# First layer's attention of a two-layer decoder: rows of two blocks, scores ahead of their maxima, group 2's factor in its probabilities

## The chip, the cores and the metric

The kernel runs on one core of one Trainium2 chip as one launch. The metric is the device time of the launch in microseconds, the median of the runs shown. The engines are called by the names of the profile: PE (TensorE: matmuls; PEld: its weight loads), DVE (VectorE), ACT (ScalarE), POOL (GpSimd) and SP (SyncE, which issues most transfers). Each takes its own instructions in the order of the program and waits on the others by semaphores. Matmul results land in PSUM, of which there are eight banks of 512 floats per partition here; everything else lives in SBUF.

## The reference, cut to what matters

The trunk has two layers on a residual stream of 512 rows and 1024 columns. The change touches the attention of the first layer alone: twelve heads of 64 in three groups of four. Group 0 sees the 128 rows before, group 1 takes every fourth row, group 2 every sixteenth. Each group has its own softmax, and the groups are weighed against each other by their softmax denominators.

```python
def banded_attention(q, k, v, n_back):
    ...
    s = jnp.where(mask[None, :, None], s, NEG)
    m = jnp.max(s, axis=-1, keepdims=True)
    p = jnp.exp(s - m)
    l = jnp.sum(p, axis=-1, keepdims=True)
    o = jnp.einsum('nbhqk,nbkhd->nbqhd', (p / l).astype(v.dtype), vc)
    lse = (m + jnp.log(l))[..., 0]

def dilated_mixer(xn, w_qkv, w_o, cos, sin):
    ...
    alpha = jax.nn.softmax(jnp.stack(lses, axis=0), axis=0)
    o = jnp.concatenate([outs[g] * alpha[g][..., None].astype(outs[g].dtype)
                         for g in range(len(A_GROUPS))], axis=2)
    return o.reshape(B, T, A_WIDTH) @ w_o
```

## The kernel before

Large products run as three matmuls each on a number split into a high and a low part (lines 290 to 292, `mm3`); the high part is a copy on ACT, the low part a subtraction on DVE. Weights are loaded by SP, split ahead of use (`W`, lines 60 and 78, or 64 and 82 where a gain is multiplied in), and taken in order.

The attention is worked through in four projections one after the other. `v_proj0` makes group 0's values. `wide_proj(1, ...)` and `wide_proj(2, ...)` make queries and keys of groups 1 and 2, and a last `wide_proj` the values of both. A `wide_proj` holds four PSUM banks from its start to its end, one for each block of 128 rows, and runs four rounds of 24 matmuls. Behind each round a row of a table names what is put between the rounds: this table is the order of the work. Four banks are left for everything in the rows:

- `qk_transpose(g, b)`: four transposes of the queries and keys of block b into a bank (qkT_ps), copied to SBUF by DVE.
- `scores(g, b)`: for each half `hh` of the heads a bank (s_ps) with two heads' scores (lines 1141 and 1143; K is 64, so the two halves lie on different rows of PE's array), then for each head `softmax`: one DVE instruction scales, masks and takes the maximum (line 1126), one ACT instruction takes the exponential and its sum (line 1127). The probabilities are in `p`, the statistics in `st`.
- `p_transpose(g, b)`: the probabilities of a block transposed into a bank (pT_ps, line 1163) and copied to SBUF by ACT.
- `next(sums)`, `next(down0)`: a step of another job, four DVE subtractions (dsums, lines 593 to 596) that prepare the down projection's weights, with their loads and stores on SP.

`factors` (line 1187 on) works out each group's weight from the statistics and spreads each group's factor to 64 columns (`fac`, line 1198: DVE for group 0, POOL for groups 1 and 2). Behind the last projection comes what is called the tail here: `pv` multiplies probabilities and values (o_ps, lines 1212 and 1215; 64 output rows a head, two halves of the array side by side), and ACT copies the result to SBUF (`ow`); `weigh` transposes the factor (f_ps, line 1228) and DVE multiplies (line 1230); `combine` splits the product into high and low part (OT, lines 1236 and 1237). Groups 1 and 2 are kept in the regrouped order of rows until `pv` copies them back. The tail ends where the output projection begins (acc, `Proj`), which takes eight banks and group 0's OT first, groups 1 and 2 some 11 us later; in its middle it calls `late`.

Of the kernel before, what the change touches and what calls it, by code (L numbers as in the profile page):

```python
# [9 lines left out]
F32 = mybir.dt.float32  # L10
F32R = mybir.dt.float32r
BF16 = mybir.dt.bfloat16
AF = mybir.ActivationFunctionType
# [104 lines left out]
def trunk_kernel(ctx, tc, x, norm_gains, w_qkv_a, w_o_a, w_q_b, w_o_b, kv_norm, w_kvf, b_f,  # L118
# [1007 lines left out]
        dve.tensor_tensor_reduce(p, s, mask, -0.125, BIG, ALU.add, ALU.min, keep[:, hd:hd + 1])  # L1126
        act.activation(p, p, AF.Exp, bias=keep[:, hd:hd + 1], scale=-1.0, accum_out=keep[:, 4 + hd:5 + hd])

    def scores(g, b):
        q = qkT[g]  # L1130

        k0 = 0 if (g == 0 and b) else 1
        n = 256 if g == 0 else 128
        p = None
        for hh in range(2):
            hs_ = slice(64 * hh, 64 * hh + 64)
            o = bank([128, 2, n], name="s_ps")
            for pr in range(2):
                if g == 0:
                    ov = o[:, pr, k0 * 128:].rearrange("p (k c) -> p k c", c=128)  # L1140
                    pe.matmul(ov, q[hs_, b, pr, :], q[hs_, b - 1 + k0:b + 1, 2 + pr, :], start=True, stop=True)
                else:
                    pe.matmul(o[:, pr, :], q[hs_, b, pr, :], q[hs_, b, 2 + pr, :], start=True, stop=True)
            if g == 0 or hh == 0:
                p = t2([128, 512 // n, n], name="p")
                P[g, b, hh] = p
            for pr in range(2):
                if g == 0:
                    softmax(g, b, 2 * pr + hh, o[:, pr, k0 * 128:], mask0[:, k0 * 128:], p[:, pr, k0 * 128:])
                else:  # L1150
                    softmax(g, b, 2 * pr + hh, o[:, pr, :], mask0[:, 128:256] if g == 1 else mask2,
                            p[:, 2 * hh + pr, :])

    def p_transpose(g, b):
        if b == 0:
# [25 lines left out]
    def factors():  # L1181
# [11 lines left out]
        dve.tensor_tensor(mn, mn, w[:, 2], ALU.add)  # L1193
        dve.reciprocal(mn, mn)
        dve.tensor_tensor(f, f, mn[:, None].to_broadcast([128, 3, 4, 4]), ALU.mult)
        for g in range(3):
            fac[g] = t4([128, 4, 4, HD], name="fac")
            (pool.tensor_copy if g else dve.tensor_copy)(fac[g], f[:, g, :, :, None].to_broadcast([128, 4, 4, HD]))

# [2 lines left out]
    def pv(g, pr):  # L1202
        o = bank([128, T], name="o_ps")
        for b in range(4):
            for hh in range(2):
                hd = 2 * pr + hh
                ov = o[64 * hh:64 * hh + 64, b * 128:(b + 1) * 128]
                vs = slice(hd * 64, hd * 64 + 64)
                if g == 0:
                    ks = [0, 1] if b else [1]  # L1210
                    for k in ks:
                        pe.matmul(ov, V[g][:, b - 1 + k, vs], PT[g][hh][:, b, 2 * pr + k, :],
                                  start=k == ks[0], stop=k == 1)
                else:
                    pe.matmul(ov, V[g][:, b, vs], PT[g][0][:, b, 2 * hh + pr, :], start=True, stop=True)
        ow[g, pr] = t = t2([128, T], name="ow")
        if g == 0:
            act.copy(t, o)
# [13 lines left out]
    def combine(g, pr):  # L1232
        t = ow.pop((g, pr))
        if pr == 0:
            OT[g] = t8([128, 2, 2, T], F32R, name=f"OT{g}")
        act.copy(OT[g][:, 0, pr, :], t)
        dve.tensor_tensor(OT[g][:, 1, pr, :], t, OT[g][:, 0, pr, :].bitcast(F32), ALU.subtract)

    def v_proj0(between):
        banks = []  # L1240
# [160 lines left out]
    v_proj0([[L(qk_transpose, 0, 0), L(qk_transpose, 0, 1), L(next, down0)],  # L1401
             [L(qk_transpose, 0, 2), L(qk_transpose, 0, 3), L(scores, 0, 0), L(scores, 0, 1), L(next, sums), L(next, down0)]])
# [16 lines left out]
    for g in range(2):  # L1419
        for pr in range(2):  # L1420
            pv(g, pr)
    weigh(0, 0)
    weigh(0, 1)
    combine(0, 0)
    pv(2, 0)
    pv(2, 1)
    weigh(1, 0)
    combine(0, 1)
    weigh(1, 1)
    combine(1, 0)  # L1430
    weigh(2, 0)
    combine(1, 1)
    weigh(2, 1)

    rows = load_conv(0)
    grow = t2([16, 128], name="g_rows")
# [3 lines left out]
    cp = []  # L1440

    def late():
        combine(2, 0)
        combine(2, 1)
# [406 lines left out]
```

## Time and profile before

| | us |
|---|---|
| median of three runs | 1103.31 (1102.62 to 1103.96) |
| the profiled execution | 1103.35 |
| its span, first to last instruction | 1101.6 |
| queries and keys of groups 1 and 2, values, with their rows | 47 to 131 |
| the tail, to the first matmul of the output projection | 131 to 141.8 |

All instructions after the output projection are the same in both kernels. The page gives each engine's busy time and the chain that ended last; a timeline lists rows of equal instructions with their start, the time from the first start to the last end, engine, line, operation, what is written and read, and in brackets how long the engine was idle before and what released it. PE's instructions overlap, so that there the distance from one start to the next counts, and not the duration. PE's clock was granted at 0.998 of full speed throughout.

### The profile page before, as it was taken

How to read it: one execution, taken by the hardware profiler on the slowest of the kernel's cores; microseconds unless marked ns; L12 is line 12 of the kernel's file. 1: busy time of each engine (PE TensorE's matmuls, PEld its weight loads, DVE VectorE, ACT ScalarE, POOL GpSimd, SP SyncE). 2: the span in 40 equal slices, each digit the busy share in tenths (PEclk: the TensorE clock that was granted, in tenths of full speed). 3: DMA queues.
4: the chain of work that ended last, by engine and by line, in shares of the span. 5: the costliest groups of instructions: out<-in, count | busy, mean ns of one | idle time of the engine just before them, and what ended most of it. 6: DMA issues, size and time to landing. Idle time of an engine off the chain costs nothing.

```text
span 1101.6 us, 18104 instructions
## 1 busy us (share of the span) xinstructions
PE 1093.7 (99%) x6608; PEld 951.8 (86%) x6608; DVE 877.1 (80%) x1498; ACT 670.4 (61%) x1114; POOL 174.2 (16%) x247
## 2 busy tenths in 40 slices
PE   9999999999999999999999999999999999999997
PEld 6988889899999988888878888889899999988886
DVE  5897788888788679997587667868888788779894
ACT  6754565756666647576552488755656666647572
POOL 3632001311111211000000212101311111211000
PEclk9999999999999999999999999999999999999999
DMA  9799854477987979894446867784468888989872
GB/s 316 205 359 408 312 168 136 90 184 187 212 193 182 247 255 321 306 321 119 134 154 219 268 187 198 233 263 135 87 180 193 206 190 183 238 269 321 308 249 77
DMA packets 192130, 242.67 MB, mean 220 GB/s; under 512 B 12848, under 2 KB 138792, under 8 KB 192040
## 3 DMA queue, kind: packets, MB, share of 16 engines
q1 hardware_dynamic: 176408, 189.33, 53.0%
q0 software_dynamic: 14944, 52.18, 20.7%
q8 instruction: 52, 0.85, 0.3%
q14 instruction: 38, 0.31, 0.1%
q10 hardware_dynamic: 688, 0.01, 0.0%
HBM read 172.37 MB, written 39.73 MB: 193 GB/s over the span
## 4 chain that ended last, share of the span: by engine, by line
PE 97%; DMA 1%; DVE 1%; issue 0%; ACT 0%; DVEq 0%
PE up L292 12%; PE up L291 12%; PE up L290 12%; PE acc L290 9%; PE acc L292 9%; PE acc L291 9%; PE v_ps L292 2%; PE v_ps L290 2%; PE v_ps L291 2%; PE qk_ps L1305 2%; PE pT_ps L1692 2%; PE o_ps L1707 2%; PE s_ps L1658 2%; PE first L292 1%; PE first L290 1%; PE first L291 1%
## 5 line engine op out<-in xcount | busy, mean ns | idle before, releaser
L290 PE MATMUL acc<-w 128*128 128x512 f32 (+1 forms) x311 | 120.6, 388 | 0.3 <-DVE mix L339 0.3
L292 PE MATMUL acc<-w 128*128 128x512 f32 (+1 forms) x311 | 120.4, 387 | 0.0
L291 PE MATMUL acc<-w 128*128 128x512 f32 (+1 forms) x267 | 103.2, 387 | 0.0
L78 DVE TENSOR_TENSOR w<-wraw,w 128x1024 fp32r<-128x1024 f32 x62 | 82.3, 1346 | 22.2 <-ACT w L60 21.8
L292 PE MATMUL up<-xsh,w 128*128 128x256 f32 x352 | 99.7, 283 | 0.1
L290 PE MATMUL up<-xsh,w 128*128 128x256 f32 x352 | 99.6, 283 | 0.0
L291 PE MATMUL up<-xsl,w 128*128 128x256 f32 x352 | 99.6, 283 | 0.0
L627 ACT ACTIVATE bb<-up,conv 128x512 f32<-128x512 f32 x80 | 59.6, 775 | 59.4 <-DVE up L1014 48.6
L60 ACT CAST w<-wraw 128x1024 fp32r<-128x1024 f32 x81 | 83.3, 1049 | 17.3 <-PE v_ps L291 6.9
L291 PE MATMUL up<-xbl,w 128*128 128x512 f32 (+1 forms) x276 | 93.5, 339 | 0.0
L291 PE MATMUL up<-xcl,w 128*128 128x512 f32 (+1 forms) x276 | 93.5, 339 | 0.0
L292 PE MATMUL up<-xbh,w 128*128 128x512 f32 (+1 forms) x276 | 93.5, 339 | 0.0
L290 PE MATMUL up<-xch,w 128*128 128x512 f32 (+1 forms) x276 | 93.5, 339 | 0.0
L290 PE MATMUL up<-xbh,w 128*128 128x512 f32 (+1 forms) x276 | 93.5, 339 | 0.0
L292 PE MATMUL up<-xch,w 128*128 128x512 f32 (+1 forms) x276 | 93.4, 338 | 0.0
L290 PEld LDWEIGHTS acc<-w 128*128 128x128 f32 x311 | 58.4, 188 | 12.4 <-DVE mix L339 0.7
L292 PEld LDWEIGHTS acc<-w 128*128 128x128 f32 x311 | 58.4, 188 | 12.0
L292 PEld LDWEIGHTS up<-xsh,w 128*128 128x128 f32 x352 | 67.6, 192 | 0.3 <-DMA w<-wsum 0.3
L291 PEld LDWEIGHTS up<-xsl,w 128*128 128x128 f32 x352 | 67.6, 192 | 0.0
L290 PEld LDWEIGHTS up<-xsh,w 128*128 128x128 f32 x352 | 67.6, 192 | 0.0
L628 DVE SCALAR_TENSOR_TENSOR bb<-up,conv,bb 128x511 f32<-128x511 f32 x80 | 59.5, 744 | 5.9 <-ACT bb L627 5.8
L630 DVE SCALAR_TENSOR_TENSOR bb<-up,conv,bb 128x510 f32<-128x510 f32 x80 | 59.9, 748 | 2.8
(313 smaller groups left out, 3109.1 us busy)
## 6 DMA issues: line engine op xcount, KB each, us to landing
wraw<-in_w_up_dram SPq DMA_DIRECT2D x88, 512.0 KB
w<-wraw POOLq DMA_DIRECT2D x32, 512.0 KB, 6.4
dT<-dsums SPq DMA_DIRECT2D x28, 512.0 KB
w<-wsum POOLq DMA_DIRECT2D x24, 512.0 KB, 5.7
dsums<-in_w_down_dram SPq DMA_DIRECT2D x22, 512.0 KB
dsums<-in_w_down_dram SPq DMA_DIRECT2D x44, 256.0 KB
hD<-hc POOLq DMA_DIRECT2D x44, 256.0 KB, 6.7
dact<-hD SPq DMA_DIRECT2D x44, 256.0 KB
```

Of the source, the lines that this page charges most:

```text
L60: (copy or self.nc.scalar.copy)(pair[:, 0], raw)
L78: self.nc.vector.tensor_tensor(pair[:, 1], raw, pair[:, 0].bitcast(F32), ALU.subtract)
L290: pe.matmul(o, ah, bh, start=first, stop=False, skip_group_check=shared)
L291: pe.matmul(o, ah, bl, start=False, stop=False, skip_group_check=shared)
L292: pe.matmul(o, al, bh, start=False, stop=last, skip_group_check=shared)
L627: act.activation(bb[:, s, :], ps, AF.Identity, bias=cp[:, 3, ch:ch + 1], scale=cp[:, 2, ch:ch + 1])
L628: dve.scalar_tensor_tensor(bb[:, s, 1:], ps[:, :T - 1], cp[:, 1, ch:ch + 1], bb[:, s, 1:], ALU.mult, ALU.add)
L630: dve.scalar_tensor_tensor(bb[:, s, 2:], ps[:, :T - 2], cp[:, 0, ch:ch + 1], bb[:, s, 2:], ALU.mult, ALU.add)
L1305: pe.matmul(qk_banks[b], a[n == 2], w[n == 1][:, kc % 2, :], start=kc + n == 0, stop=kc + n == KD + 1)
L1658: pe.matmul(sc[j, i][hh][:, :nn], qT[j][own, qp, i * 128:(i + 1) * 128], k[own, kp, :nn], start=qp + kp == 0, stop=qp == 1)
L1692: pe.transpose(o[:, k0 + k, :], p[:, hh, k * 128:(k + 1) * 128], ident)
L1707: pe.matmul(o[64 * hh:64 * hh + 64, i * 128:(i + 1) * 128], Vt[hd // 8][:, k, (hd % 8) * 64:(hd % 8) * 64 + 64], pT[j, i, hh][:, k, :], st ...
```

## The change

- `scores` takes several blocks. All their matmuls are issued first, into banks that for groups 1 and 2 hold both blocks of a half (two banks for two blocks, and not four), and all maxima and exponentials follow.
- The tables put two blocks' scores or two blocks' transposes in a row. The last row of each `wide_proj` is left empty or has no PE work.
- `factors` multiplies group 2's factor into its probabilities `p` (four DVE multiplications of 128x512), and spreads a factor for groups 0 and 1 alone. It stands one row earlier.
- Group 2 is transposed in the tail, its product is not copied to `ow` and not weighed; `combine` splits it straight from PSUM, in regrouped order.
- Group 2's values are scaled and copied by ACT, as group 1's are, and not by DVE.
- The tail's order is new, and `combine(2, ...)` moves from `late` into it.

```diff
-    def scores(g, b):
-        q = qkT[g]
-
-        k0 = 0 if (g == 0 and b) else 1
+    def scores(g, *blocks):
+        q, todo = qkT[g], []
         n = 256 if g == 0 else 128
...
+        if g:
+            both = [bank([128, 2, 2, n], name="s_ps") for _ in range(2)]
+        for b in blocks:
+            k0 = 0 if (g == 0 and b) else 1
+            p = None
+            for hh in range(2):
+                hs_ = slice(64 * hh, 64 * hh + 64)
+                o = both[hh][:, b % 2] if g else bank([128, 2, n], name="s_ps")
...
+                    else:
+                        todo.append((g, b, 2 * pr + hh, o[:, pr, :], mask0[:, 128:256] if g == 1 else mask2,
+                                     p[:, 2 * hh + pr, :]))
+        for a in todo:
+            softmax(*a)
...
-        for g in range(3):
+        for b in range(4):
+            p = P[2, b, 0].rearrange("p (h r) c -> p h r c", h=2)
+            fb = f[:, 2, b].rearrange("p (r h) -> p h r", h=2)[:, :, :, None].to_broadcast([128, 2, 2, 128])
+            dve.tensor_tensor(p, p, fb, ALU.mult)
+        for g in range(2):
             fac[g] = t4([128, 4, 4, HD], name="fac")
             (pool.tensor_copy if g else dve.tensor_copy)(fac[g], f[:, g, :, :, None].to_broadcast([128, 4, 4, HD]))
...
+        if g == 2:
+            ow[g, pr] = o
+            return
         ow[g, pr] = t = t2([128, T], name="ow")
...
-        act.copy(OT[g][:, 0, pr, :], t)
-        dve.tensor_tensor(OT[g][:, 1, pr, :], t, OT[g][:, 0, pr, :].bitcast(F32), ALU.subtract)
+        hi, lo = (OT[g][:, part, pr, :] for part in range(2))
+        if g == 2:
+            t = t.rearrange("p (r l) -> p r l", r=4)
+            hi, lo = (a.rearrange("p (l r) -> p r l", r=4) for a in (hi, lo))
+        act.copy(hi, t)
+        dve.tensor_tensor(lo, t, hi.bitcast(F32), ALU.subtract)
...
-        dve.tensor_scalar(V[2][:, b, :], o[:, 256:512], factor(2, b), None, ALU.mult)
+        act.activation(V[2][:, b, :], o[:, 256:512], AF.Identity, scale=factor(2, b))
...
     wide_proj(1, "qk_ps", qk_post, [
-        [L(p_transpose, 0, 0)],
-        [L(scores, 0, 2), L(scores, 0, 3), L(p_transpose, 0, 1), L(next, sums)],
-        [L(p_transpose, 0, 2), L(next, sums)],
-        [stat_out, L(p_transpose, 0, 3), L(next, sums)]])
+        [L(p_transpose, 0, 0), L(p_transpose, 0, 1)],
+        [L(scores, 0, 2, 3), L(next, sums)],
+        [L(p_transpose, 0, 2), L(p_transpose, 0, 3), L(next, sums)],
+        [stat_out, L(next, sums)]])
...
-        [L(qk_transpose, 1, 2), L(scores, 1, 0), L(scores, 1, 1)],
-        [L(qk_transpose, 1, 3), L(p_transpose, 1, 0)],
-        [L(scores, 1, 2), L(scores, 1, 3), L(p_transpose, 1, 1), stat_in]])
+        [L(qk_transpose, 1, 2), L(qk_transpose, 1, 3), L(scores, 1, 0, 1)],
+        [L(p_transpose, 1, 0), L(p_transpose, 1, 1), L(scores, 1, 2, 3)],
+        [stat_in]])
...
-        [L(qk_transpose, 2, 0), L(qk_transpose, 2, 1), L(p_transpose, 1, 2)],
-        [L(qk_transpose, 2, 2), L(qk_transpose, 2, 3), L(scores, 2, 0), L(scores, 2, 1), L(p_transpose, 1, 3)],
-        [L(scores, 2, 2), L(scores, 2, 3), L(p_transpose, 2, 0)],
-        [factors, L(p_transpose, 2, 1), L(p_transpose, 2, 2), L(p_transpose, 2, 3)]])
-    for g in range(2):
-        for pr in range(2):
-            pv(g, pr)
+        [L(p_transpose, 1, 2), L(p_transpose, 1, 3), L(qk_transpose, 2, 0), L(qk_transpose, 2, 1)],
+        [L(qk_transpose, 2, 2), L(qk_transpose, 2, 3), L(scores, 2, 0, 1)],
+        [L(scores, 2, 2, 3), factors],
+        []])
+    pv(0, 0)
+    pv(0, 1)
     weigh(0, 0)
     weigh(0, 1)
+    for b in range(4):
+        p_transpose(2, b)
     combine(0, 0)
+    pv(1, 0)
+    pv(1, 1)
...
+    combine(1, 0)
     pv(2, 0)
     pv(2, 1)
...
     combine(1, 1)
-    weigh(2, 1)
+    combine(2, 0)
+    combine(2, 1)
```

The first place is PE behind the second round of the value projection (v_ps), where group 2's first scores stand; the numbers behind names are those of the buffers. Before:

```order
L292 MATMUL v_ps<-w,xpl_147 128x512
L1116 MATMUL qkT_ps<-ident,qk_1126 128x128 x8
L1143 MATMUL s_ps<-qkT_1249 128x128 x8
L1163 MATMUL pT_ps<-ident,p 128x128 x4
L290 MATMUL v_ps<-w,xph_146 128x512
```

Now:

```order
L292 MATMUL v_ps<-w,xpl_147 128x512
L1116 MATMUL qkT_ps<-ident,qk_1158 128x128 x8
L1145 MATMUL s_ps<-qkT_1257 128x128 x8
L290 MATMUL v_ps<-w,xph_146 128x512
L291 MATMUL v_ps<-w,xph_146 128x512
```

The transposes of group 1's last probabilities have moved a row ahead; the scores are as many, in two banks.

The second place is DVE between group 2's last maxima and the tail: the factors (f_mn, f_f, f_w), the weight's low part (w), the sums (dsums) and the weighing (ow). Before:

```order
L596 TENSOR_TENSOR dsums<-dsums 128x512
L78 TENSOR_TENSOR w<-wraw,w 128x1024
L1398 TENSOR_SCALAR V_1446<-v_ps,rt 128x256 x4
L1187 TENSOR_TENSOR f_mn<-st 128x16
L1188 TENSOR_TENSOR f_mn<-f_mn,st 128x16
L1189 TENSOR_TENSOR f_f<-f_mn,st 128x48
L1191 TENSOR_TENSOR f_w<-st,f_f 128x48
L1192 TENSOR_TENSOR f_mn<-f_w 128x16
L1193 TENSOR_TENSOR f_mn<-f_mn,f_w 128x16
L1194 RECIPROCAL f_mn<-f_mn 128x16
L1195 TENSOR_TENSOR f_f<-f_f,f_mn 128x48
L1198 COPY fac<-f_f 128x1024
```

Now, from the last step of the factors on:

```order
L1199 TENSOR_TENSOR f_f<-f_f,f_mn 128x48
L1203 TENSOR_TENSOR p<-p,f_f 128x512 x4
L1206 COPY fac<-f_f 128x1024
L593 TENSOR_TENSOR dsums<-dsums 128x512
L594 TENSOR_TENSOR dsums<-dsums 128x512
L595 TENSOR_TENSOR dsums<-dsums 128x512
L596 TENSOR_TENSOR dsums<-dsums 128x512
L78 TENSOR_TENSOR w<-wraw,w 128x1024
L1241 TENSOR_TENSOR ow<-ow,f_ps 128x4x128 x2
L1252 TENSOR_TENSOR OT_1551<-ow,OT_1551 128x512 x2
```

The factors come ahead of the sums and the low part, with four multiplications of p ahead of the copy, and the values of group 2 are gone from DVE.

The third place is PE in the tail, from the end of group 0's products. Before (twelve transposes of group 2's probabilities stand ahead of group 0's products):

```order
L1212 MATMUL o_ps<-PT_1_676,V_507 64x128 x2
L1215 MATMUL o_ps<-PT_0_1096,V_1445 64x128 x16
L1228 MATMUL f_ps<-ident,fac 128x128 x8
L1215 MATMUL o_ps<-PT_0_1421,V_1446 64x128 x16
L1228 MATMUL f_ps<-ident,fac 128x128 x16
L290 MATMUL acc<-w,OT_1579 128x512
```

Now:

```order
L1220 MATMUL o_ps<-PT_1_676,V_507 64x128 x2
L1239 MATMUL f_ps<-ident,fac 128x128 x8
L1167 MATMUL pT_ps<-ident,p 128x128 x16
L1223 MATMUL o_ps<-PT_0_1094,V_1450 64x128 x16
L1239 MATMUL f_ps<-ident,fac 128x128 x8
L1223 MATMUL o_ps<-PT_0_1526,V_1451 64x128 x16
L290 MATMUL acc<-w,OT_1551 128x512
```

Group 0's factor is transposed right behind group 0's products, group 2's probabilities follow, and the eight transposes of group 2's factor are gone. A row of sixteen products is 32 passes in the profile, a row of eight scores sixteen.

More of the change, by code (lines that the diff above doesn't have):

```diff
@@ new lines, in scores @@
+        if g:
[6 more added lines that the diff above has]
+                o = both[hh][:, b % 2] if g else bank([128, 2, n], name="s_ps")
+                for pr in range(2):
+                    if g == 0:
+                        ov = o[:, pr, k0 * 128:].rearrange("p (k c) -> p k c", c=128)
+                        pe.matmul(ov, q[hs_, b, pr, :], q[hs_, b - 1 + k0:b + 1, 2 + pr, :], start=True, stop=True)
+                    else:
+                        pe.matmul(o[:, pr, :], q[hs_, b, pr, :], q[hs_, b, 2 + pr, :], start=True, stop=True)
+                if g == 0 or hh == 0:
+                    p = t2([128, 512 // n, n], name="p")
+                    P[g, b, hh] = p
+                for pr in range(2):
+                    if g == 0:
+                        todo.append((g, b, 2 * pr + hh, o[:, pr, k0 * 128:], mask0[:, k0 * 128:], p[:, pr, k0 * 128:]))
+                    else:
+                        todo.append((g, b, 2 * pr + hh, o[:, pr, :], mask0[:, 128:256] if g == 1 else mask2,
+                                     p[:, 2 * hh + pr, :]))
@@ L1397, in v_post @@
         act.activation(V[1][:, b, :], o[:, 0:256], AF.Identity, scale=factor(1, b))
-        dve.tensor_scalar(V[2][:, b, :], o[:, 256:512], factor(2, b), None, ALU.mult)
+        act.activation(V[2][:, b, :], o[:, 256:512], AF.Identity, scale=factor(2, b))
     down0 = down_sums([*[(0, j) for j in range(ND)], (1, 8)], in_one, sp, 1, 1)
     v_proj0([[L(qk_transpose, 0, 0), L(qk_transpose, 0, 1), L(next, down0)],
-             [L(qk_transpose, 0, 2), L(qk_transpose, 0, 3), L(scores, 0, 0), L(scores, 0, 1), L(next, sums), L(next, down0)]])
+             [L(qk_transpose, 0, 2), L(qk_transpose, 0, 3), L(scores, 0, 0, 1), L(next, sums), L(next, down0)]])
@@ L1442, in late @@
     def late():
-        combine(2, 0)
-        combine(2, 1)
         cp.append(conv_columns(rows))
```

27 lines of the change are left out of this document (3 added, 24 removed).

## The prediction

> **What bounds the kernel now.** The page's first part and its chain of waits come first, then the list of waits of TensorE over the stage that the change touches (44 to 178 us).
>
> ```profile
> PE 1093.7 (99%) x6608; PEld 951.8 (86%) x6608; DVE 877.1 (80%) x1498; ACT 670.4 (61%) x1114; POOL 174.2 (16%) x247
> PE 97%; DMA 1%; DVE 1%; issue 0%; ACT 0%; DVEq 0%
> PE pT_ps L1163 <- DVE st L1126: 0.2, 1, 0.2
> ```
>
> TensorE is busy for 1093.7 us and makes 97% of the chain; in the whole stage one wait of 0.2 us is named. So a microsecond counts only if it is one of TensorE's own, and these are read from the starts of its rows: the time from one start to the next is what a row costs in the queue, while the durations overlap.
>
> **The change part by part.**
>
> *Eight transposes go.* Group 2's factor moves into its probabilities, so its two weighing steps vanish, each with four transposes into f_ps. The tail of the stage:
>
> ```profile
> 130.72 1.47 PE L1163 MATMUL pT_ps<-ident,p 128*128 128x128 f32 x12
> 132.12 3.33 PE L1212 MATMUL o_ps<-PT,V 128*64 128x128 f32 x56
> 135.22 1.97 PE L1215 MATMUL o_ps<-PT,V 128*64 128x128 f32 x32
> 137.12 1.09 PE L1228 MATMUL f_ps<-ident,fac 128*128 128x128 f32 x8
> 138.15 1.97 PE L1215 MATMUL o_ps<-PT,V 128*64 128x128 f32 x32
> 140.04 1.96 PE L1228 MATMUL f_ps<-ident,fac 128*128 128x128 f32 x16
> 141.76 0.48 PE L290 MATMUL acc<-w,OT 128*128 128x512 f32 x1
> ```
>
> Sixteen transposes take 141.76 - 140.04 = 1.72 us, 0.108 each; eight are **-0.86**.
>
> *Waits inside the rows go.* A visit of sixteen score passes that waits for nothing is this one; it lasts 101.86 - 100.66 = 1.20 us.
>
> ```profile
> 100.34 0.39 PE L292 MATMUL qk_ps<-w,xpl 128*128 128x512 f32 x1
> 100.66 1.26 PE L1143 MATMUL s_ps<-qkT 64*128 64x128 f32 x16
> 101.86 0.66 PE L1163 MATMUL pT_ps<-ident,p 128*128 128x128 f32 x4
> 102.27 0.47 PE L290 MATMUL v_ps<-w,xph 128*128 128x512 f32 x1
> 102.58 0.39 PE L291 MATMUL v_ps<-w,xph 128*128 128x512 f32 x1
> ```
>
> The other three of the same form last longer, because with four banks held by the projection a visit that takes four banks of scores, behind or ahead of transposes, must wait for VectorE to empty one:
>
> ```profile
> 87.12 1.56 PE L1143 MATMUL s_ps<-qkT 64*128 64x128 f32 x16
> 88.61 0.50 PE L290 MATMUL qk_ps<-w,xph 128*128 128x512 f32 x1
> 88.95 0.40 PE L291 MATMUL qk_ps<-w,xph 128*128 128x512 f32 x1
> ...
> 115.61 1.72 PE L1143 MATMUL s_ps<-qkT 64*128 64x128 f32 x16
> 117.27 0.66 PE L1163 MATMUL pT_ps<-ident,p 128*128 128x128 f32 x4
> ...
> 123.33 1.26 PE L1143 MATMUL s_ps<-qkT 64*128 64x128 f32 x16
> 124.75 0.66 PE L1163 MATMUL pT_ps<-ident,p 128*128 128x128 f32 x4 [0.16 <-DVE st L1126]
> 125.16 0.47 PE L290 MATMUL v_ps<-w,xph 128*128 128x512 f32 x1
> ```
>
> They are 1.49, 1.66 and 1.42 us, so 0.29 + 0.46 + 0.22 = 0.97 of waiting. Group 0 has one more: eight transposes behind its scores against eight alone.
>
> ```profile
> 60.93 1.32 PE L1163 MATMUL pT_ps<-ident,p 128*128 128x128 f32 x8
> 62.00 0.47 PE L290 MATMUL qk_ps<-w,xph 128*128 128x512 f32 x1
> ...
> 80.02 0.39 PE L292 MATMUL qk_ps<-w,xpl 128*128 128x512 f32 x1
> 80.26 1.03 PE L1116 MATMUL qkT_ps<-ident,qk 128*128 128x128 f32 x8
> 81.36 0.40 PE L291 MATMUL qk_ps<-w,xph 128*128 128x512 f32 x1
> ```
>
> 1.07 us against eight at 0.108 less the overlap of the last (0.79) and 0.06 of entry leaves 0.22. In the changed order no row holds more than two kinds, groups 1 and 2 take two score banks in place of four, and no probabilities are transposed right behind scores, so I let all four go: **-1.19**; the bounds are nothing and 1.19.
>
> *Changes of kind on TensorE.* Transposes alone between projection matmuls are free: from 80.02 to 81.36 is 1.34 us, which eight at 0.108 and two matmuls at 0.23 ((130.72 - 125.16) / 24) fill. So merging two such visits gains nothing. Scores are not free to enter and leave (100.34 to 100.66 is 0.09 over a matmul's 0.23, 88.61 to 88.95 is 0.11 over), and behind them transposes were a cheap way out: scores, four transposes, matmul cost 0.41 + 0.31 us after the scores (101.86, 102.27, 102.58), apart 0.34 + 0.43. That is +0.05 for each of four visits (group 0's second, group 1's second, both of group 2). In the tail, eight transposes between value products take 138.15 - 137.12 = 1.03 (0.16 over eight at 0.108), 32 product passes before them 137.12 - 135.22 = 1.90 (0.16 over 32 at 3.10 / 56 each, about 0.055). Before there are four such changes, and the ends were cheap, since transposes stood at both (132.12 - 130.72 is 0.1 over twelve, 141.76 - 140.04 nothing over sixteen). Afterwards products stand at both ends: one more change to products, 0.16, and a way out to the projection, for which I take the scores' 0.09 + 0.11. Together **+0.56**, between 0.2 (the four visits alone) and 0.8.
>
> *What now hangs on VectorE.* Ahead of the copy of group 0's factor come four new multiplications of 128x512, and behind it the sums for w_down and a weight's low part, which stood ahead of the factors. TensorE needs that copy early: group 0's factor is transposed right behind group 0's products. These are the steps, first VectorE's, then ScalarE's, then GpSimd's.
>
> ```profile
> 124.18 0.29 DVE L1126 CUSTOM_DVE_ANT_0 p<-s_ps,mask 128x128 f32<-128x128 f32 x1 [1.44 <-PE s_ps L1143]
> 125.88 0.69 DVE L593 TENSOR_TENSOR dsums<-dsums 128x512 f32<-128x512 f32 x1
> 129.17 1.23 DVE L78 TENSOR_TENSOR w<-wraw,w 128x1024 fp32r<-128x1024 f32 x1 [0.42 <-ACT w L60]
> 132.81 0.21 DVE L1191 TENSOR_TENSOR f_w<-st,f_f 128x48 f32<-128x48 f32 x1 [0.31 <-ACT f_f L1190]
> 134.00 0.69 DVE L1198 COPY fac<-f_f 128x1024 f32<-128x1024 f32 x1
> 137.89 2.23 DVE L1230 TENSOR_TENSOR ow<-ow,f_ps 128x512 f32<-128x512 f32 x2 [3.20 <-PE f_ps L1228]
> 139.99 0.67 DVE L1237 TENSOR_TENSOR OT<-ow,OT 128x512 fp32r<-128x512 f32 x1
> ...
> 124.52 0.40 ACT L1127 ACTIVATE p<-p,st 128x128 f32<-128x128 f32 x1 [3.03 <-DVE st L1126]
> 127.62 0.56 ACT L1165 COPY PT<-pT_ps 128x512 f32<-128x512 f32 x1
> ...
> 134.03 2.54 POOL L1198 COPY fac<-f_f 128x1024 f32<-128x1024 f32 x2 [26.06 <-DVE f_f L1195]
> ```
>
> From group 2's last scores to the factor's transposes TensorE needs 1.20 (visit) + 5.56 (24 matmuls, 125.16 to 130.72) + 0.1 + 3.10 (132.12 to 135.22) + 0.16 = 10.1 us. VectorE's side: the first maximum started 0.85 us after the first score; as two blocks now share a bank and it waits for both, 1.25 (the visit's row ends 1.26 after its start). Then 0.34 to the first exponential, 3.10 for eight (124.52 to 127.62), 0.31 for the factors' own, 1.19 to the factors (132.81 to 134.00), four multiplications at 0.70 (the sums' form, two operands in SBUF), 0.69 of copy: 9.7. It just fits. But GpSimd's copy of group 1's factor starts with the same release, 2.54 / 2 = 1.27 us, and beside GpSimd's copies VectorE has been slow:
>
> ```profile
> 29.79 4.49 DVE L82 SCALAR_TENSOR_TENSOR w<-wearly,gcol,w 128x256 fp32r<-128x256 f32 x4
> 30.20 1.28 POOL L1090 CAST xph<-xah 128x512 fp32r<-128x512 f32 x1
> ```
>
> Four operations of only 128x256 took 1.12 us each, at the pace of the casts, where half a 0.70 would be 0.35; one multiplication meets one copy and loses about 0.8. Next in VectorE's queue are four sums (2.8), a low part (1.2) and two weighings (139.99 - 137.89 = 2.1), and by the program's waits group 2's products need a bank which the second weighing frees. TensorE gets there 24 transposes (2.6), 32 passes (1.75), eight transposes (0.87) and three changes (0.48) later, 5.7 us against VectorE's 6.1. So VectorE is late there by 9.7 + 0.8 + 6.1 - 10.1 - 5.7 = 0.8, and 0.1 of handing over: **+0.9**, between 0.1 (no loss to GpSimd) and 2.3 (multiplications as dear as a weighing, 1.05).
>
> The Trainium skill (SBUF — State Buffer, "SBUF: two separate sides") says that VectorE with two SBUF inputs and GpSimd take turns on a shared port pair for whole instructions. The pace above agrees with it. By its letter one multiplication would wait for a whole copy, 1.27 in place of 0.8, and the sum would be 0.0 in place of -0.5; a rival below is this case.
>
> *The rest.* Group 2's values on ScalarE: four evictions more at the row's end, under the 3.10 us of group 0's products, at 0.4 each (1.6 us); uncovered they would delay group 1's products. Group 2's result is split straight from PSUM in regrouped order, as a weighing is (1.05 against 0.7); it holds two banks longer while the output projection takes its eight: **+0.1**, between 0 and 0.4. Sixteen moved transposes of group 2 cost what they cost before. SP issues the same transfers in the same order and GpSimd one copy less; the sums for w_down come some 6 us later, so their stores, and the loads of weights behind these in SP's queue, do too, which is free as long as the loads run as far ahead as they do (in this stage TensorE names no wait for a transfer). After 178 us the order of all engines is as it was.
>
> Sum: -0.86 - 1.19 + 0.56 + 0.9 + 0.1 = -0.5 us. The profiled execution took 1103.35 us (its span and 1.7 around it), so 1102.85; the median of the runs shown is 0.04 lower: **1102.8 us**.
>
> **The rivals.**
>
> *VectorE is never waited for.* GpSimd's copy meets nothing, the split of group 2 frees its banks in time, and the changes of kind come out even (half of them are my extrapolation from scores to products): -0.86 - 1.19 = -2.05, **1101.3**. For it: the chain fits without GpSimd. Against it: the second meeting of VectorE and TensorE is 0.1 short even then. Chance 0.28, a bit under half of it past 0.2%.
>
> *VectorE's chain becomes the bound.* Place: the first factor transpose, which stands in TensorE's queue ahead of everything in the tail. If all four multiplications run like the row at 29.79, 1.12 plus 0.35 for the other half, they take 5.9 in place of 3.6: +2.3, **1105.1**. The gain is gone from 1.03 us a multiplication (4.1 for four), and past 1.58 the loss exceeds 0.2%. For it: a row of the same kernel; against it: one GpSimd copy there, not four. Chance 0.15.
>
> *One multiplication blocked for the whole copy.* Then 1.27 in place of 0.8, the rest as in the sum: -0.5 + 0.5, **1103.3**, no gain; the change then does not do what a count of its instructions says. For it: the casts' pace; against it: part of an operation there seems to lie beside the cast (1.12 against 1.28). Chance 0.1. The Trainium skill's rule from the page named above, taken at its word, is this case.
>
> **How the numbers follow.** The forecast has 0.37, the three rivals 0.28, 0.15 and 0.1, what I have not seen 0.1. What this kernel's measurement can tell from no change is about 0.2%, 2.2 us: faster than 1101.1 are 0.13 of the first rival and half of the unseen, 0.18; slower than 1105.5 are 0.07 of the second and the other half, 0.12; the rest, 0.7, lies between. The range reaches a little past the first rival, where half of what lies beyond 0.2% stays out, and past the second: 1100.6 to 1105.3; the forecast's own, by the bounds of its waits on VectorE (0.1 to 2.3 for 0.9), is 1102.0 to 1104.2.
>
> **What would show it.** Right: 24 transposes into f_ps become 16; score visits of 1.2 us everywhere; f_ps or group 2's o_ps released by VectorE after a gap of half a microsecond or so; one of the four multiplications near 1.5 us. Wrong: a score visit still at 1.4 or more (a bank is still short), f_ps without a gap (first rival), four multiplications over 1 us (second), or gaps after 178 us.

## The result, and the profile after

| | before | after |
|---|---|---|
| median, twenty runs each (us) | 1103.49 (1102.49 to 1104.11) | 1101.67 (1100.91 to 1102.61) |
| span of the profiled execution | 1101.6 | 1099.8 |
| start of the first transposes of queries and keys | 44.66 | 44.95 |
| from there to the first matmul of the output projection, called the stretch below | 97.10 | 95.74 |
| from that matmul to the end | 959.80 | 959.11 |

The ratio is 0.9985, with a 95% interval of 0.9979 to 0.9992: 1.8 us faster, 0.9 to 2.3. The forecast was 0.5 us faster, 1102.8 us. The rows below are those that answer to the prediction's. First the page's engine line, then TensorE's timeline of the changed kernel: the visits of scores, and the tail.

```profile
PE 1092.0 (99%) x6600; PEld 951.0 (86%) x6600; DVE 877.4 (80%) x1496; ACT 671.1 (61%) x1116; POOL 174.4 (16%) x246
```

```profile
87.57 1.26 PE L1145 MATMUL s_ps<-qkT 64*128 64x128 f32 x16
88.76 0.50 PE L290 MATMUL qk_ps<-w,xph 128*128 128x512 f32 x1
...
115.70 1.26 PE L1145 MATMUL s_ps<-qkT 64*128 64x128 f32 x16
116.90 0.50 PE L290 MATMUL v_ps<-w,xph 128*128 128x512 f32 x1
...
122.58 1.26 PE L1145 MATMUL s_ps<-qkT 64*128 64x128 f32 x16
123.77 0.50 PE L290 MATMUL v_ps<-w,xph 128*128 128x512 f32 x1
...
129.45 3.33 PE L1220 MATMUL o_ps<-PT,V 128*64 128x128 f32 x56
132.77 1.09 PE L1239 MATMUL f_ps<-ident,fac 128*128 128x128 f32 x8
133.70 1.91 PE L1167 MATMUL pT_ps<-ident,p 128*128 128x128 f32 x16
135.54 1.97 PE L1223 MATMUL o_ps<-PT,V 128*64 128x128 f32 x32
137.80 1.06 PE L1239 MATMUL f_ps<-ident,fac 128*128 128x128 f32 x8 [0.30 <-DVE ow L1241]
138.79 1.97 PE L1223 MATMUL o_ps<-PT,V 128*64 128x128 f32 x32
140.69 0.50 PE L290 MATMUL acc<-w,OT 128*128 128x512 f32 x1
```

Every visit of sixteen score passes lasts 1.19 to 1.20 us (88.76 - 87.57, 116.90 - 115.70, 123.77 - 122.58), where three of them lasted 1.42 to 1.66. The transposes of factors are 16, not 24. In the tail one wait is named: 32 products of group 1 and their way out take 137.80 - 135.54 = 2.26 us, where 32 of group 2 take 1.90 (140.69 - 138.79). So 0.36 us is lost there, on VectorE. These are VectorE's rows in that time, then GpSimd's:

```profile
128.77 3.34 DVE L1203 TENSOR_TENSOR p<-p,f_f 128x512 f32<-128x512 f32 x4
132.03 0.68 DVE L1206 COPY fac<-f_f 128x1024 f32<-128x1024 f32 x1
132.63 0.68 DVE L593 TENSOR_TENSOR dsums<-dsums 128x512 f32<-128x512 f32 x1
...
135.41 1.22 DVE L78 TENSOR_TENSOR w<-wraw,w 128x1024 fp32r<-128x1024 f32 x1
136.54 2.15 DVE L1241 TENSOR_TENSOR ow<-ow,f_ps 128x512 f32<-128x512 f32 x2
...
128.80 1.56 POOL L1206 COPY fac<-f_f 128x1024 f32<-128x1024 f32 x1 [18.76 <-DMA wraw<-in_w_o_a_dram]
```

And the view of the one line 1203 (shortest, median and longest in ns):

```profile
L1203 DVE TENSOR_TENSOR p<-p,f_f x4: 677/686/1523, 128.8 to 131.4; 128x512 f32<-128x512 f32 x4
```

The four multiplications take 132.03 - 128.77 = 3.26 us from start to start; three are of 0.68 and one of 1.52. The copy of group 0's factor ends at 132.71 and TensorE reads it from 132.77. The first weighing starts at 136.54 only, behind four sums and a low part, and takes half of 2.15: it ends at about 137.6, and group 1's transposes start at 137.80. The second ends at 138.69, and the row of PE's weight loads for group 2's products names a weighing too:

```profile
138.79 0.74 PEld L1223 LDWEIGHTS o_ps<-PT,V 128*64 128x64 f32 x14 [0.17 <-DVE ow L1241]
```

### The profile page after: what moved, and what is told of

The parts are those of the page before. It is cut to its first block, busy times and chain, and to the rows that moved or that the text cites. A ratio compares the mean times of both kernels' runs of the same rounds, so it can differ in the third digit from the quotient of the medians.

```text
span 1099.8 us, 18080 instructions
## 1 busy us (share of the span) xinstructions
PE 1092.0 (99%) x6600; PEld 951.0 (86%) x6600; DVE 877.4 (80%) x1496; ACT 671.1 (61%) x1116; POOL 174.4 (16%) x246
## 4 chain that ended last, share of the span: by engine, by line
PE 99%; DVE 1%; issue 0%; ACT 0%; DVEq 0%; ACTq 0%
PE up L291 13%; PE up L290 13%; PE up L292 13%; PE acc L290 9%; PE acc L292 9%; PE acc L291 9%; PE v_ps L290 2%; PE v_ps L292 2%; PE v_ps L291 2%; PE qk_ps L1320 2%; PE pT_ps L1708 2%; PE o_ps L1723 2%; PE s_ps L1674 2%; PE qk_ps L290 1%; PE first L292 1%; PE first L290 1%
```

## The experiments

All runs were timed beside the kernel before on the same chip (its medians were 1103.1 to 1103.2 us). As one execution differs from the next by half a microsecond and more, each kernel is judged by its stretch first, which is read from the profile, and by the time second.

| run | stretch (us) | change of the median (us) | ratio, 95% interval |
|---|---|---|---|
| before_again | 97.04 | -0.1 | 0.9990 to 1.0008 |
| after_again | 95.75 | -1.6 | 0.9976 to 0.9993 |
| rows_only | 95.90 | -1.5 | 0.9979 to 0.9997 |
| tail_only | 96.35 | -0.7 | 0.9984 to 1.0002 |
| four_banks | 96.50 | -0.8 | 0.9983 to 1.0001 |
| factor1_dve | 95.49 | -1.6 | 0.9976 to 0.9993 |
| sums_late | 95.41 | -0.1 | 0.9988 to 1.0006 |
| stores_last | 95.41 | -1.7 | 0.9975 to 0.9993 |
| all_three | 95.05 | -2.1 | 0.9972 to 0.9989 |
| values2_dve | 97.98 | +1.1 | 1.0000 to 1.0018 |
| sums_early | 99.27 | -0.2 | 0.9996 to 1.0014 |
| sums_early_again | 97.06 | +0.6 | 0.9997 to 1.0023 |

**What one execution differs by.** Both kernels unchanged.

> The kernel before, unchanged, for what differs from one execution to the next. The two profiles so far differ by 1.80 us in the span: 0.29 lost ahead of the first transposes of queries and keys (44.66 to 44.95), 1.36 gained from there to the first matmul of the output projection (97.10 to 95.74 us), 0.74 gained behind it, most of it two waits of TensorE for a weight's low part (0.4 at 386.7, 0.2 at 242.7 us). Theory 1: only the middle stretch is the change's; the two others are chance, so this profile has 97.1 +- 0.05 us in the middle and other waits behind it, by some tenths of a us. Theory 2: the change moved the transfers of the low parts out of a collision; then the waits at 386.7 and 242.7 are here again, at the same places and sizes.

> The changed kernel, unchanged. Theory 1: 95.74 +- 0.05 us in the middle stretch, some other start, and behind the output projection waits of some tenths of a us that need not be absent. Theory 2: no wait at the places of 386.7 and 242.7 us again, so 0.6 us of the gain belongs to the change though it lies behind its stage.

The stretch came out at 97.04 and 95.75: it repeats to 0.06 us, and the change gains 1.29 to 1.36 there. The two waits behind it, in the first profile of before these,

```profile
243.06 0.19 PEld L292 LDWEIGHTS up<-xbh,w 128*128 128x128 f32 x1 [0.38 <-DMA w<-wraw]
387.15 0.19 PEld L292 LDWEIGHTS up<-xsh,w 128*128 128x128 f32 x1 [0.34 <-DMA w<-wsum]
```

are not in the second, which takes 959.12 us from the output projection to the end, as the changed kernel does (959.11, 959.16). Theory 2 falls: what lies behind the stretch is not the change's, and neither is the start (44.0 to 45.1 over all profiles). So 1.3 us is the change's; the 1.8 of the medians has it inside its interval.

**The rows alone, and the tail alone.** One kernel, rows_only, has the change's tables and `scores`; the other, tail_only, has its `factors`, values, `pv`, `combine` and tail. Of each edit the last rows of the tables are shown, the first against the changed kernel, the second against the kernel before:

```diff
...
         [L(qk_transpose, 2, 2), L(qk_transpose, 2, 3), L(scores, 2, 0, 1)],
-        [L(scores, 2, 2, 3), factors],
-        []])
+        [L(scores, 2, 2, 3)],
+        [factors, *[L(p_transpose, 2, b) for b in range(4)]]])
...
```

```diff
...
         [L(qk_transpose, 2, 2), L(qk_transpose, 2, 3), L(scores, 2, 0), L(scores, 2, 1), L(p_transpose, 1, 3)],
-        [L(scores, 2, 2), L(scores, 2, 3), L(p_transpose, 2, 0)],
-        [factors, L(p_transpose, 2, 1), L(p_transpose, 2, 2), L(p_transpose, 2, 3)]])
+        [L(scores, 2, 2), L(scores, 2, 3), factors],
+        []])
...
```

> The rows and the shared score banks of the change, with group 2's factor, values, weighing and tail as before. By the prediction's terms: the waits in the score visits are gone (0.29 + 0.46 + 0.22, and 0.22 behind group 0's), four ways out cost 0.05 more each: -1.0 of 97.1 in the middle stretch, 96.1, with each visit of sixteen passes at 1.19. Rival: the waits come back elsewhere in the rows (nothing gained, 97.1), since the gain is only TensorE work moved.

> Group 2's factor in its probabilities, its values on ScalarE and the new tail, with the rows and the four score banks of before. Eight transposes fewer are -0.86, the wait of 0.22 behind the last scores goes with the transposes that stood there, changes of kind cost +0.36. Theory 1: the wait on VectorE depends on when the first maximum starts; with a bank for each block it starts 0.85 after the first score and not 1.3, so the wait of 0.36 + 0.06 shrinks to nothing: 96.3 in the middle stretch. Rival (the wait hangs on something else, as a bank that ScalarE frees): 96.7.

The rows alone gain 1.17 of 97.07 (the mean of before), nearly all that the whole change gains. The tail alone gains 0.72, as theory 1 had it (96.3), and its rows show why it gains more by itself than the 0.16 which it adds to the rows. This is TensorE in the tail of tail_only:

```profile
130.57 3.33 PE L1216 MATMUL o_ps<-PT,V 128*64 128x128 f32 x56
133.83 1.10 PE L1235 MATMUL f_ps<-ident,fac 128*128 128x128 f32 x8
...
136.61 1.97 PE L1219 MATMUL o_ps<-PT,V 128*64 128x128 f32 x32
138.50 1.09 PE L1235 MATMUL f_ps<-ident,fac 128*128 128x128 f32 x8
```

133.83 - 130.57 = 3.26 and 138.50 - 136.61 = 1.89, where the changed kernel has 3.32 and 2.26: no wait. With a bank for each block VectorE's first maximum starts at 124.56, 0.86 behind the first score, and not 1.30 behind it (122.58 to 123.88 in the changed kernel), and all that follows is that much sooner. That is 0.42 of the difference of 0.56; the rest lies within the wait of 0.22 at the last scores, which goes with either edit and counts once when both are made (that visit lasts 1.19 in tail_only too).

**Four score banks in the changed kernel.** The same thing from the other side:

```diff
-            both = [bank([128, 2, 2, n], name="s_ps") for _ in range(2)]
+            both = [[bank([128, 2, n], name="s_ps") for _ in range(2)] for _ in blocks]
...
-                o = both[hh][:, b % 2] if g else bank([128, 2, n], name="s_ps")
+                o = both[b % 2][hh] if g else bank([128, 2, n], name="s_ps")
```

> The changed kernel with a score bank for each block and half again (four in place of two); rows and order stay. Theory 1 (the waits were for banks): visits of scores behind transposes, three of them, lose 0.3 to 0.5 each again (1.19 becomes 1.5 to 1.7), the visit of scores alone stays at 1.19; in return the first maximum is 0.45 sooner and the wait of 0.36 in the tail is gone; middle stretch 95.74 + 0.9 to 1.5 - 0.4 = 96.2 to 96.8. Rival (the waits went because nothing is transposed behind scores, and all scores stand ahead of the maxima): all visits stay at 1.19, and the stretch is 95.3.

TensorE's timeline of this kernel:

```profile
87.10 1.72 PE L1145 MATMUL s_ps<-qkT 64*128 64x128 f32 x16
88.75 0.50 PE L290 MATMUL qk_ps<-w,xph 128*128 128x512 f32 x1
...
136.16 1.97 PE L1223 MATMUL o_ps<-PT,V 128*64 128x128 f32 x32
138.06 1.09 PE L1239 MATMUL f_ps<-ident,fac 128*128 128x128 f32 x8
```

The visit lasts 1.65 again, and the others behind transposes 1.43 and 1.65; the one of scores alone stays at 1.19. That is 1.16 us of waiting back, and 0.42 in the tail gone (138.06 - 136.16 = 1.90): 96.50, as theory 1 had it. The gain in the visits of scores is the banks', not that of the order of scores and maxima; and its price is the later first maximum, which the tail pays. (The 0.22 at group 0's second scores, whose banks are the same in both, is not tested by this.)

**The wait in the tail.** Two edits that bring VectorE's weighing forward: the sums behind it, or group 1's factor off GpSimd.

```diff
-            next(down0, None)
+            if not (name == "v_ps" and s >= 2):
+                next(down0, None)
...
     weigh(0, 1)
+    next(down0, None)
+    next(down0, None)
```

```diff
-            (pool.tensor_copy if g else dve.tensor_copy)(fac[g], f[:, g, :, :, None].to_broadcast([128, 4, 4, HD]))
+            dve.tensor_copy(fac[g], f[:, g, :, :, None].to_broadcast([128, 4, 4, HD]))
```

> The last sums for w_down (four VectorE operations, 2.9 us) stand behind group 0's two weighings in place of ahead of them. Theory 1: the 0.36 us that the 32 products of group 1 and their way out take over 1.90 (2.26) is a wait for VectorE's weighing; the weighings start some 2.5 us sooner, the row is 1.90 again, the middle stretch 95.74 - 0.36 = 95.4. Rival: it is what the change from products to transposes costs there; the row stays at 2.26 and the stretch at 95.7. A second rival: VectorE is only late later, and the output projection waits up to 2.9 us for a low part of OT; the stretch is 95.4 and the loss stands right behind it.

> Group 1's factor is copied by VectorE behind group 0's, and no longer by GpSimd beside the four multiplications. Theory 1 (the two engines share a port): all four multiplications take 0.60 us from start to start, not one of them 1.45; group 0's factor is there 0.84 sooner, which TensorE can use for 0.06, and the weighings come 0.84 - 0.68 = 0.2 sooner, so the wait of 0.36 falls to about 0.15; the middle stretch is 95.5. Rival (the second multiplication is slow of itself, by its data or its place): 1.45 stays, VectorE is 0.68 later, the stretch grows by 0.7 to 96.4.

With the late sums the stretch is 95.41, 0.34 less: the wait was for the weighing. With the factor on VectorE it is 95.49, 0.25 less: the 32 products of group 1 and their way out take 2.01 us (from 134.53 to 136.54), so 0.11 of the wait is left, much as theory 1 had it. VectorE's rows of factor1_dve:

```profile
127.82 2.49 DVE L1203 TENSOR_TENSOR p<-p,f_f 128x512 f32<-128x512 f32 x4
130.23 1.29 DVE L1206 COPY fac<-f_f 128x1024 f32<-128x1024 f32 x2
```

Four multiplications now take 130.23 - 127.82 = 2.41 from start to start, 0.60 each, in place of 3.26: what one lost beside GpSimd's copy is 0.85, and the rival (slow of itself) falls. The Trainium skill (SBUF — State Buffer, "SBUF: two separate sides") has the two engines take turns on a shared port pair for a whole instruction; the trace agrees, with both sides of it. GpSimd's copy began 0.03 us after the first multiplication and took 1.56 us, and the second multiplication lost 0.85, about what was left of the copy when the first had ended (129.46 to 130.36). The kernel before shows the copy's own price, of which the prediction's 1.27 is no more than a mean:

```profile
L1198 POOL COPY fac<-f_f x2: 1035/1296/1557, 134.0 to 135.5; 128x1024 f32<-128x1024 f32 x2
```

The first copy, of 1.56, started with VectorE's own copy of a factor (134.00); the second, with VectorE idle, took 1.04.

The late sums did not make the kernel faster, though (1102.97 us). The second rival was near: a loss came later, but by SP and not by VectorE. These are SP's rows of the changed kernel, then those of sums_late, then ScalarE's and TensorE's of sums_late:

```profile
134.07 1.77 SPq L601 DMA_DIRECT2D dT<-dsums  x2
139.41 1.06 SPq L50 DMA_DIRECT2D wraw<-in_w_o_a_dram  x2
```

```profile
137.41 1.77 SPq L601 DMA_DIRECT2D dT<-dsums  x2
143.67 0.90 SPq L50 DMA_DIRECT2D wraw<-in_w_o_a_dram  x2
```

```profile
149.66 1.05 ACT L60 CAST w<-wraw 128x1024 fp32r<-128x1024 f32 x1 [3.04 <-DMA wraw<-in_w_o_a_dram]
...
166.34 1.32 PE L361 MATMUL xt_ps<-ident,xn 128*128 128x128 f32 x8 [0.26 <-DVE xn L311]
```

SP's store of the sums waits for the sums, and the loads of weights stand behind it in SP's queue, 4.3 us later (143.67 against 139.41). ScalarE waits 3.04 us for one, its casts come where the norm's work should be, and the stage behind the output projection starts 36.09 us after the projection's first matmul in place of 35.42: 0.7 lost. (Another 0.4 is lost at 693 us, in the second layer; waits of the same line came in two other profiles and were absent in the rest.) The medians differ by more, 1102.97 against 1101.46 for after_again; what the executions that were not profiled lost beyond this is not shown. In the next run, against the changed kernel too, the last stores alone come later than with the late sums:

```diff
...
     weigh(0, 1)
+    next(down0, None)
...
     def late():
+        next(down0, None)
```

> As with the late sums, and the last stores to the down projection's sums stand on SP behind the two weight loads of the output projection in place of ahead of them (and the stores before those behind one load). Theory 1: the late sums cost 0.7 us at the boundary only because SP's stores waited for them and held the loads back; now the stretch is 95.4 as there, ScalarE does not wait 3 us for a weight, the boundary does not wait: 1101.5 - 0.4 = 1101.1. Rival (VectorE itself is too late for the boundary, since the sums took the place of something): the wait at the boundary is there again.

SP's loads now start at 137.74. The stretch is 95.41, nothing is lost behind it (959.09 us to the end), the median 1101.38: theory 1.

**Sums earlier.** One step more in an empty row should do both at once, and did not.

```diff
-        [stat_in]])
+        [stat_in, L(next, down0)]])
```

> The changed kernel with the sums for w_down one round earlier (one step more in the empty row of groups 1 and 2), so that none stands between factors and weighings and SP's stores and loads come earlier, not later. Theory 1: the row of group 1's products is 1.90, the middle stretch 95.4 as with the late sums, and behind it none of that run's waits (0.7 at the boundary of the output projection, where ScalarE waited 3.0 us for a weight that SP issued 3.3 us later): 1101.5 - 0.4 = 1101.1. Rival: VectorE's additional 2.9 us ahead of group 2's scores delay the copies of its queries and keys, and the scores wait for them.

A miss by 4 us, and the rival's mechanism is near: VectorE first waits for loads, since a step's sums now follow the step that issues their load too closely. The timeline of VectorE and TensorE, then TensorE by windows (from and to, length, busy time, granted clock, DMA share, GB/s):

```profile
109.77 0.69 DVE L593 TENSOR_TENSOR dsums<-dsums 128x512 f32<-128x512 f32 x1 [3.40 <-DMA dsums<-in_w_down_dram]
...
114.72 0.69 DVE L593 TENSOR_TENSOR dsums<-dsums 128x512 f32<-128x512 f32 x1 [0.88 <-DMA dsums<-in_w_down_dram]
...
134.59 1.30 PE L1239 MATMUL f_ps<-ident,fac 128*128 128x128 f32 x8 [2.19 <-DVE fac L1206]
135.69 3.41 PE L1167 MATMUL pT_ps<-ident,p 128*128 128x128 f32 x16
```

```profile
131.92:135.33 3.41, 1.22 (x16) 1.00 0.00 0
135.34:138.74 3.40, 3.40 (x19) 0.50 0.07 19
138.75:142.16 3.41, 3.41 (x47) 1.00 0.62 147
```

Group 2's last maxima and the factors are late by what VectorE lost, TensorE idles 2.19 us for group 0's factor, and then sixteen transposes take 3.34 us where they took 1.84: the clock was granted at half.

**Group 2's values on VectorE.** The edit that the prediction put at nothing, undone in the changed kernel, with TensorE's rows behind it:

```diff
-        act.activation(V[2][:, b, :], o[:, 256:512], AF.Identity, scale=factor(2, b))
+        dve.tensor_scalar(V[2][:, b, :], o[:, 256:512], factor(2, b), None, ALU.mult)
```

> The changed kernel with group 2's values on VectorE again. The prediction put this edit at nothing as long as it is covered. Theory 1: on VectorE the four evictions would stand behind factors, multiplications, sums and a low part, and TensorE's transposes of group 2's probabilities need the banks that they free: the first comes free at 136.9 in place of 128.9, the transposes at 133.7 wait some 3 us, and after such a gap the clock is granted at half for 3 us (as in the run of the early sums): stretch 95.74 + 4 to 5 = 100. Theory 2: only VectorE's 1.65 us count, by which the weighing is later: 97.4. Rival: there is room, 95.7.

```profile
133.48 1.04 PE L1167 MATMUL pT_ps<-ident,p 128*128 128x128 f32 x8
136.86 1.09 PE L1167 MATMUL pT_ps<-ident,p 128*128 128x128 f32 x8 [2.34 <-DVE V L1413]
```

The place is theory 1's: TensorE waits for banks that VectorE's evictions free. It is at the third block's transposes (eight had banks), so 2.24 us are lost and not 3, and no half clock followed: the stretch is 97.98 and not 100. The other theories, which have no such wait, fall.

> The kernel with the early sums, a second profile. In the first TensorE idled 2.2 us ahead of group 0's factor and then ran 3.4 us at half the granted clock, while a gap of 2.3 us (group 2's values on VectorE) had no such sequel. Theory A: whether the clock is halved depends on how the gap lies to a time grid of the chip, so it differs from run to run: this profile may show the gap of 2.2 us alone, with a middle stretch of 99.27 - 1.7 = 97.6. Theory B: it follows from the place (transposes behind the gap, no work of TensorE in between): 99.3 again.

This profile has a gap of 1.64 us and full clock in all windows behind it; the stretch is 97.06. By itself that does not decide between A and B, since the gap was shorter; the gap of 2.34 above, also ahead of transposes and without a sequel, speaks against length alone and against B. The last section reads the three gaps against the clock's own steps, which bear out A.

**A kernel that beats both.** Late sums, the stores behind the loads, the factor on VectorE, and group 1's factor transposed next to group 2's probabilities (`weigh` is cut in its transposes and its multiplication, here `times`; of the edit, the order of the tail is shown):

```diff
...
     weigh(0, 0)
     weigh(0, 1)
+    times(0, 0)
+    times(0, 1)
+    next(down0, None)
     for b in range(4):
         p_transpose(2, b)
+    weigh(1, 0)
+    weigh(1, 1)
...
-    weigh(1, 0)
-    weigh(1, 1)
+    times(1, 0)
+    times(1, 1)
...
```

> Late sums with the stores behind the loads, group 1's factor copied by VectorE, and group 1's factor transposed right behind group 2's probabilities, so that the products of groups 1 and 2 are one run of 64. Each part by what the runs before showed: -0.36 (wait for the weighing), -0.06 (wait for group 0's factor), and two changes of kind fewer: eight transposes between products took 0.99 + 0.15 on the last pass where 0.87 of them is theirs, -0.27. Middle stretch 95.74 - 0.69 = 95.05, 1101.5 - 0.7 = 1100.8. Rival: a bank is short (the eight that the tail has are all in use at once), and a new wait takes the 0.27 back: 95.3 or more.

```profile
129.60 3.33 PE L1220 MATMUL o_ps<-PT,V 128*64 128x128 f32 x56
132.86 1.10 PE L1239 MATMUL f_ps<-ident,fac 128*128 128x128 f32 x8
133.79 1.91 PE L1167 MATMUL pT_ps<-ident,p 128*128 128x128 f32 x16
135.54 1.04 PE L1239 MATMUL f_ps<-ident,fac 128*128 128x128 f32 x8
136.51 3.71 PE L1223 MATMUL o_ps<-PT,V 128*64 128x128 f32 x64
140.15 0.50 PE L290 MATMUL acc<-w,OT 128*128 128x512 f32 x1
```

32 transposes stand in one row, 64 products run as one, no wait is left: 95.05 as expected, 1100.97 us, 0.998 of before (0.9972 to 0.9989).

## Why the prediction was right, and where it was not

The time lies in the range, on the side of gain that was forecast, but outside the narrower 1102.0 to 1104.2 which the forecast gave for itself: the gain in the stretch is 1.3 us where 0.5 was said, and the other half microsecond of the medians' 1.8 is not shown to be the change's. Term by term:

- **Eight transposes, -0.86.** Right: 16 f_ps transposes are left, at 0.109 each. No run takes them out alone; in tail_only, where the tail has no wait, -0.86, -0.22 at the last scores and +0.36 for the changes of kind make the -0.72 that was measured.
- **Waits in the rows, -1.19, and ways out of scores, +0.2.** Right in kind and size: -1.0 forecast, -1.17 in rows_only. four_banks shows the cause, the banks.
- **Changes of kind in the tail, +0.36.** The tail lasts from its last projection matmul to the second one behind it 11.90 us after and 11.60 before, with four transposes fewer (0.44): 0.74 more, of which 0.42 are waits. That leaves 0.32. Right.
- **VectorE, +0.9.** This is the term that was mis-sized: 0.42. Both meetings were there, and so was the slow multiplication (1.52 where "near 1.5" was said). VectorE's chain was priced too dear. Multiplications were put at 0.70, their duration; on VectorE, too, the distance from start to start counts, 0.60, and the four took 3.26 with the loss to GpSimd where 3.6 was said. So the copy of group 0's factor ended 10.13 us behind the last scores' start and not 10.5, and the first meeting cost 0.06; the second weighing ended 16.1 behind it and not 16.6. The second meeting cost 0.36, one row ahead of where the text had it: group 1's factor transposes wait for the first weighing (the row at 137.80), presumably for a bank. The text's place, group 2's products behind the second weighing, was a wait as well: without the loss ahead of them the products would have come 0.36 sooner, at 138.43, and waited for the weighing that ended at 138.69. So naming the later place changed the sum little. That 0.8 for the meeting with GpSimd was close to 0.85 is partly luck: it came from the mean of the row at 29.79, 1.12, in which one operation took 0.75 and three 1.31 to 1.35.
- **Group 2 split from PSUM, +0.1.** Nothing: the output projection starts with no wait.
- **The sums, their stores and the loads behind them: "free as long as the loads run as far ahead".** True, and no more than that: SP's loads for the output projection were issued at 139.41 (135.48 before), and 4.3 us more cost 0.7 in sums_late.
- **Values on ScalarE, nothing.** Right, and needed: on VectorE they cost 2.24, by their banks, which the text did not see.

Of the rivals, the first (VectorE never waited for, 1101.3) is nearest in time, nearer than the forecast by the medians and hardly nearer by the stretch (2.05 and 0.5 said, 1.3 measured), and its mechanism is wrong: VectorE was waited for twice. The second's price (1.12 and more for each multiplication) and the third's (1.27 lost) did not come: one multiplication lost 0.85.

## What to carry to other kernels

Where a full TensorE waits inside a short visit, count the PSUM banks that the visit and its neighbours hold: two blocks in one bank removed every such wait of the scores here, at the price of a later start of the engine that empties them. Before an operation is moved on one engine, follow what its result releases on the queues of others: a store that waits for it holds up every load behind it on SP, and four late sums on VectorE cost 0.7 us of TensorE's time some 28 us later. Price a run of operations by the distance between starts, on VectorE as on TensorE, not by their durations.

## What was not expected of the hardware

A wait of TensorE can cost more than its length. In the profile of sums_early a gap of 2.19 us was followed by 3.41 us at half the granted clock, 1.7 us lost. Gaps of 2.34 (values2_dve) and 1.64 us (sums_early_again) had no such sequel. Of nineteen timed runs of the kernel with the early sums (sums_early and sums_early_again), eleven lie at 1101.8 to 1103.4 and eight at 1104.1 to 1107.4, as if it came in some executions only; the two that were profiled took 1104.82 and 1102.81.

The traces record when the granted clock changes, and that tells more than the lengths. In sums_early full clock begins at 5.63 us and falls at 135.34, and half the clock lasts until 138.75: the first time, 129.71 us, is 38 times the second, 3.413. In the other thirteen traces full clock lasts 1092.27 or 1088.85 us, until TensorE runs out of work: 320 or 319 of the same steps. So there is a grid, with its own start in every execution. Cut along it, the other two gaps look like this (values2_dve, then sums_early_again):

```profile
132.23:135.64 3.41, 2.29 (x22) 1.00 0.30 121
135.65:139.05 3.40, 2.19 (x30) 1.00 0.60 215
```

```profile
131.44:134.85 3.41, 1.77 (x23) 1.00 0.01 5
```

TensorE idled 2.19 of 3.41 us in the step that half the clock followed (131.92 to 135.33, above). The gap of 2.34 is divided by an end of a step, so that no step idled more than 1.21; that of 1.64 lies in one step. Over all fourteen traces every step at full clock that idled 1.99 us or more was followed by half the clock (fifteen steps, one in mid-program, the others at the end), and none that idled 1.64 or less. So in these traces a gap's place on the grid counts beside its length, as theory A had it; what lies between 1.64 and 1.99 no run shows. The start of the stretch goes with the grid too: full clock from 4.53 us and 44.00 in factor1_dve, 5.82 and 44.66 in before, 6.70 and 45.10 in sums_late (four_banks, 4.31 and 44.48, does not fit).

The Trainium skill (TensorE: Matmul & The Clock Gate, "What's actually happening") says that the clock is set by a monitor with a window of some 3.4 us that runs freely, and that the clock falls after an idle window of that length. The step of 3.413 us and its free start agree. A window idle throughout was not needed here: 1.99 of 3.41 us was enough, and the measurement decides.
